# Experts' inputs: the first gathering from unsplit fp32 rows, the split parts made one pair later, two gate pieces requested earlier

## The chip, the cores and the metric

The kernel runs on one core of a Trainium2 chip. A core has a matrix engine (TensorE, PE in the profile, with its weight loads as PEld), a vector engine (VectorE, DVE), a scalar engine (ScalarE, ACT), GpSimd (POOL) and SyncE (SP), which here issues most transfers; sixteen DMA engines move the data. The metric is the device time of one execution in microseconds (us), lower is better. The given number is the median of three executions.

## The reference

The program is a small network over 256 tokens of width 1024: four layers of a first block, then two layers of a second block (layer 0 and layer 1 below). Only the end of each second-block layer matters here, its two-level mixture of experts:

```python
g_w, g_idx = lax.top_k(softmax(xf @ w_group + b_group), 1)          # one of 4 groups
e_val, e_idx = lax.top_k(e_logits of that group, 2)                 # two of its 4 experts
gates = sum(one_hot(g_idx * 4 + e_idx) * g_w * softmax(e_val))
for e in range(16):
    hid = silu(xt @ w_gate[e]) * (xt @ w_up[e])                     # 1024 -> 512
    y = y + gates[:, e:e + 1] * (hid @ w_down[e])                   # 512 -> 1024
```

All weights are fp32: 2 MB for each of the three matrices of an expert, 96 MB for the sixteen experts of a layer. Its input `xt` is a normalised, scaled and shifted copy of the layer's state.

## The kernel before, in words

**The order of the work.** The kernel is written with tile pools: a tool turns the Python program into one instruction queue for each engine, adds the waits, and chooses the order within each queue from a simulated timeline, with the order of the program as priority. Each queue runs in order. `aside`, `tick` and `settle` weave the steps of one small chain between those of another; `behind(x)` keeps an engine's instructions behind `x`. A tile is allocated from a pool under a name with a number of buffers (`one(shape, name, bufs=...)` in the stage's own pool, `wt` for the weight buffers raw, whi and wlo with four each, `xp` for xTh and xTl with two each); a buffer that is asked for again has to wait until its last reader is done, and so does a transfer into it, with all that stands behind it on SP's queue.

**The experts' stage** (`second_layer`, `moe_pass`). The tokens of an expert are gathered with matmuls: a 0/1 matrix `Dm` (128 tokens x 128 places) is made by comparing slots with an iota, and the token rows `X` (tokens on partitions) are the stationary operand, 128 features at a time. The experts are worked off in eight pairs j = 0..7 (one of the groups 0 and 1, one of the groups 3 and 2); a gathering serves two pairs, so there are four in a layer (q = 0..3), each of 4 x 2 x 2 x 2 = 32 matmuls (feature blocks, halves of the tokens, parts) of 256 columns (`collect`, line 1675). `shifted` moves the result from PSUM into `xg` on ACT (8 instructions of 128x256).

**Parts.** A row is scaled by its norm and split: `hi` is the value rounded to the engine's one-pass format fp32r, `lo` the rest. Two fp32r matmuls, with `hi` and `lo`, add up to the exact row. `parts(h)` makes both from `xG[h]`, ACT the first (line 2038), DVE the second (line 2039). The feature order is changed on the way: feature p * 8 + k goes to column k * 128 + p, because the expert weights are loaded so that each partition holds eight neighbouring rows. So the scaling reads at a stride of 8 elements, writes contiguously, and the gathering's stationary operand is contiguous.

**The routing** ahead of the first pair, for the two token halves h: update of the state, transposes, logits against the router's weights (line 2027), `route` (a chain of about a dozen short DVE instructions that finds group and experts), `route_slots` (matmuls that count earlier tokens with the same expert, line 1627), `picks` (line 1642), the first gathering with both halves apart, and `room` (counts, line 1723). `R.whose`, which `room` makes, is read by TensorE's sequencer into eight registers (line 1838) before the first expert matmul.

**A pair** (`moe_pass`, line 1829 for its matmuls in plain fp32, four experts' strips side by side): gate, up, product `t` on ACT and DVE, transposes (line 1746), down, then `leave` and in the next pair `combine` (line 1763). In pair 1 and pair 5 the next gathering (q + 1) and its place matmuls (`put`, lines 1773 and 1776) stand between the combining and the transposes; in pair 3 they stand at the end, behind a branch (line 1961) for the case that an expert has more tokens than places, which needs the parts X too and isn't taken here.

**The weights.** `expert_weights(l, name, j)` requests the four pieces (1 MB each) of one matrix of pair j. Gate pieces go to raw, but pieces 0 and 1 of odd pairs to the two xTl buffers; up goes to whi, down to wlo. Gate 0 is requested before the stage, up 0 and down 0 at its start, and those of pair j + 1 behind the matmuls of the same name of pair j. The buffer `next` holds a row for the work after the stage, loaded early.

Of the kernel before, what the change touches and what calls it, by code (L numbers as in the profile page):

```python
# [11 lines left out]
F32 = mybir.dt.float32  # L12
F32R = mybir.dt.float32r
# [3 lines left out]
OP = mybir.AluOpType  # L17
# [4 lines left out]
D = 1024  # L22
# [6 lines left out]
HALVES = (slice(0, 512), slice(512, 1024))  # L29
# [23 lines left out]
class Net:  # L53
# [1591 lines left out]
    def gather(self, R, X, sh, q, first=False):  # L1645
# [21 lines left out]
        return Dm, xg  # L1667

    def collect(self, p, X, Dm, b, halves):

        for i in range(2):
            ks = slice((2 * b + i) * 128, (2 * b + i + 1) * 128)
            for h in halves:
                for part in range(2):
                    self.nc.tensor.matmul(p[:, i], X[h][part][:, ks], Dm[:, h].rearrange("p c s -> p (c s)"),  # L1675
                                          start=h == i == part == 0, stop=h == part == 1, skip_group_check=True)

# [109 lines left out]
    def expert_weights(self, l, name, j):  # L1787


        e = [self.expert(j, s) for s in range(2)]  # L1790
        src = self.a[f"moe_w_{name}_2"][l, e[0]:e[1] + 1:e[1] - e[0]]
        pieces = []
        for i in range(4):
            if name != "down":
                tag, n, k0 = "raw" if name == "gate" else "whi", slice(0, 512), 2 * i
                s = src.rearrange("s (p i k) n -> i p s k n", i=4, k=2)[i]
            elif j < 7:
                tag, n, k0 = "wlo", slice(0, D), i
                s = src[:, 128 * i:128 * i + 128].rearrange("s (k p) n -> p s k n", k=1)
            else:  # L1800
                tag, n, k0 = "wlo", HALVES[i // 2], 2 * (i % 2)
                s = src[:, 128 * k0:128 * k0 + 256, n].rearrange("s (k p) n -> p s k n", k=2)
            if name == "gate" and j % 2 and i < 2:
                t = self.xp.tile([128, 2, 2, 512], F32, name="xTl", tag="xTl", bufs=2)
            else:
                t = self.wt(tag, [128, 2, 1 if tag == "wlo" and j < 7 else 2, n.stop - n.start], F32)
            if name == "down" and j == 7:
                for e in range(2):
                    self.nc.sync.dma_start(t[:, e], s[:, e])
            else:  # L1810
                self.nc.sync.dma_start(t, s)
            pieces.append((t, k0, n))
        return pieces

# [18 lines left out]
    def moe_pass(self, l, X, R, sh, g2, first, weights, rest, late, ahead):  # L1833
# [14 lines left out]
        for j in range(8):  # L1848
            q, c = divmod(j, 2)
            xT = xg[:, :, c * 128:(c + 1) * 128]  # L1850
            more = range(j + 1, min(j + 2, 8))
            g, u = self.pB([128, 512]), self.pB([128, 512])
# [21 lines left out]
            if j == 6:  # L1874
                late()
            DT, (gs,) = place[j]
            out[j] = DT, self.tm(dt=F32R), self.tm(dt=F32R)
            for yn, n in zip(y, HALVES):
                left = self.leave(yn, n, gs, g2, *out[j][1:])
            if j == 3:  # L1880

                self.combine(acc, range(2), j, *out.pop(j))
                rest(acc)
                Dm, xg = self.whole(self.gather(R, X, sh, q + 1))
                put(q + 1)
# [4 lines left out]
    def moe_rest(self, l, X, R, sh, g2, base, acc):  # L1890
# [15 lines left out]
        for j in range(8):  # L1906
# [6 lines left out]
            for b in range(4):  # L1913
                p = self.pB([128, 2, 128])
                for i in range(2):
                    ks = slice((2 * b + i) * 128, (2 * b + i + 1) * 128)
                    for k in range(4):
                        h, part = divmod(k, 2)
                        nc.tensor.matmul(p[:, i], X[h][part][:, ks], Dm[:, h], start=k == 0, stop=k == 3)
                self.shifted(p, xg, b, sh)  # L1920
# [18 lines left out]
    def moe(self, l, X, R, sh, g2, first, weights):  # L1939


        nc, v = self.nc, self.nc.vector
        row = self.one([128, D], "next")

        def late():
            self.bcast(self.a["final_norm_g_2"] if l else self.mod[1, D:2 * D], D, row)

# [10 lines left out]

        def rest(acc):
            n = nc.values_load(R.most, min_val=0, max_val=8)  # L1960
# [25 lines left out]

        return update, row

    def second_layer(self, l, mix, oT, after):
# [3 lines left out]
        wr, sh, row = self.routing[l]  # L1993
        y, begin, end = self.mixed(mix, oT, w, (l, 1 - l))
        weights = {"gate": self.expert_weights(l, "gate", 0)}
        g1, G = self.mod_row(l, 2), self.mod_row(l, 4)
        with self.phase(f"moe{l}", 1, 4):
            R = self.route_start()
            g2 = self.bcast(self.mod[l, 5 * D:6 * D], D, self.one([128, D], "g2"))
            for name in ("up", "down"):  # L2000
                weights[name] = self.expert_weights(l, name, 0)

            X = [[self.one([128, D], f"X{h}{part}", F32R) for part in range(2)] for h in range(2)]
            xT = self.xp.tile([128, 8, S], F32, name="xT32", tag="xTh", bufs=2)
# [14 lines left out]
            def logits(h, u):  # L2019
                p = self.pB([128, 4, 128])  # L2020
                for j in range(4):
                    k = 4 * u + j
                    nc.tensor.transpose(p[:, j], xG[h][:, k * 128:(k + 1) * 128], self.ident)
                nc.scalar.copy(xT[:, 4 * u:4 * u + 4, h * 128:(h + 1) * 128], p)
                for j in range(4):
                    k = 4 * u + j
                    nc.tensor.matmul(lgs[:, h], xT[:, k, h * 128:(h + 1) * 128], wr[:, k], start=k == 0, stop=k == 7)

            r = {}
# [37 lines left out]
            self.tick(3)  # L2067
            parts(1)
            self.settle(chain)
# [312 lines left out]
```

## Time and profile before

| | |
|---|---|
| median of three executions | 2271.1 us (2264.89 to 2271.54) |
| the profiled execution: device time | 2268.48 us |
| its span in the trace | 2266.7 us |
| TensorE busy | 2104.9 us, 93% of the span |
| weight loads (PEld) | 1608.8 us, 71% |
| DVE, ACT, POOL busy | 1346.7 us (59%), 937.4 us (41%), 25.2 us (1%) |
| mean granted clock of TensorE | 0.973 |
| HBM read | 533.36 MB, 238 GB/s over the span |

Times in the trace count from the start of the span. The experts' stage of layer 0 has its first expert matmul at 1640.27 us, that of layer 1 at 2027.24 us. Busy time of TensorE includes the pipeline's drain of each matmul, so its share is a little too high. The granted clock is 1.0 at 2.4 GHz and 0.5 at 1.2 GHz. A piece of a chain or a timeline is given by start and duration; several instructions alike that follow each other are one row with their count; in brackets stands how long the engine was idle before, and what released it.

### The profile page before, as it was taken

To read this page: it belongs to the slowest core of one execution; us is meant where nothing else is said; L and a number is where in the kernel's file an instruction comes from. 1 tells how busy PE (TensorE), PEld (TensorE's weight loads), DVE (VectorE), ACT (ScalarE), POOL (GpSimd) and SP (SyncE) were. 2 spreads that over 40 slices of the span, in tenths; PEclk is the share of its full clock that TensorE was granted. 3 is DMA by queue.
4 is the path that set the end of the run, shared out by engine and by line. 5 is a ranking of instruction groups with operands and counts; after the bars stand their busy time and mean duration, and the time that the engine had idled before them with its cause. 6 is when DMAs were issued, how large, how long until landed. Compare 5 with 4: busy or idle time off the path is not lost. (4 is left out here: it accounts for less than half of the span.)

```text
span 2266.7 us, 35540 instructions
## 1 busy us (share of the span) xinstructions
PE 2104.9 (93%) x14072; PEld 1608.8 (71%) x14072; DVE 1346.7 (59%) x2794; ACT 937.4 (41%) x1464; POOL 25.2 (1%) x69
## 2 busy tenths in 40 slices
PE   7989999989999999999999899989898988989897
PEld 5868888976788878788888698978743327864332
DVE  4578767575877665877666787677611027851112
ACT  4545435455543455544445444446411115521111
POOL 0000000000000010000000000000000001000000
PEclk9999999999999999999999999999999998999999
DMA  8527774630587464477564387656599984469995
GB/s 296 182 74 253 268 257 171 212 121 29 191 279 278 169 217 155 173 260 267 202 229 161 87 284 261 215 205 205 225 407 418 420 353 155 152 246 420 418 419 225
DMA packets 246362, 541.67 MB, mean 239 GB/s; under 512 B 27501, under 2 KB 77189, under 8 KB 246181
## 3 DMA queue, kind: packets, MB, share of 16 engines
q1 hardware_dynamic: 242597, 533.98, 65.3%
q10 hardware_dynamic: 3552, 5.24, 0.6%
q8 instruction: 116, 1.90, 0.3%
q14 instruction: 65, 0.53, 0.1%
q0 software_dynamic: 32, 0.02, 0.0%
HBM read 533.36 MB, written 5.83 MB: 238 GB/s over the span
## 5 line engine op out<-in xcount | busy, mean ns | idle before, releaser
L289 DVE TENSOR_TENSOR wlo<-raw,whi 128x1024 fp32r<-128x1024 f32 x476 | 558.5, 1221 | 223.9 <-ACT whi L270 201.8
L270 ACT CAST whi<-raw 128x2048 fp32r<-128x2048 f32 x218 | 411.1, 1907 | 417.9 <-PE pB L308 336.8
L308 PE MATMUL pB<-whi,t 128*128 128x512 f32 x1088 | 308.1, 401 | 4.7 <-ACT t L423 3.2
L308 PE MATMUL pB<-xTl,whi 128*128 128x256 f32 x1600 | 257.0, 285 | 0.0
L308 PE MATMUL pB<-xTh,whi 128*128 128x256 f32 x1600 | 254.9, 288 | 0.4 <-ACT whi L270 0.4
L308 PE MATMUL pB<-xTh,wlo 128*128 128x256 f32 x1600 | 250.2, 284 | 0.0
L308 PEld LDWEIGHTS pB<-whi,t 128*128 128x128 f32 x1088 | 202.0, 191 | 49.0 <-ACT t L423 4.1
L308 PEld LDWEIGHTS pB<-xTh,whi 128*128 128x128 f32 x1600 | 218.8, 193 | 11.8 <-issue 8.6
L308 PEld LDWEIGHTS pB<-xTl,whi 128*128 128x128 f32 x1600 | 223.2, 193 | 5.3 <-issue 2.3
L308 PEld LDWEIGHTS pB<-xTh,wlo 128*128 128x128 f32 x1600 | 217.8, 192 | 2.7 <-issue 1.7
L308 PE MATMUL pB<-wlo,t 128*128 128x512 f32 x544 | 170.9, 395 | 0.0
L308 PE MATMUL pB<-whi,xTh 128*128 128x512 f32 (+1 forms) x512 | 145.0, 409 | 11.4 <-ACT xTh L423 9.3
L308 PE MATMUL pB<-whi,xTl 128*128 128x512 f32 (+1 forms) x512 | 143.5, 402 | 10.1 <-DVE xTl L423 6.7
L308 PE MATMUL pB<-wlo,xTh 128*128 128x512 f32 (+1 forms) x512 | 139.9, 395 | 0.0
L1195 DVE SCALAR_TENSOR_TENSOR adac<-adaw,cs,adac 128x512 f32<-128x512 f32 x168 | 125.8, 749 | 21.5 <-DMA adaw<-in_w_ada_dram 19.0
L1829 PE MATMUL pB<-wlo,t 128*32 128x512 f32 (+1 forms) x1024 | 116.6, 594 | 11.7 <-ACT t L1747 11.7
L1753 DVE SCALAR_TENSOR_TENSOR t<-pB,gs,g 128x512 f32<-128x512 f32 x32 | 24.0, 751 | 166.2 <-PE pB L1829 164.6
L308 PEld LDWEIGHTS pB<-whi,xTh 128*128 128x128 f32 x512 | 95.4, 197 | 37.2 <-ACT xTh L423 15.2
L308 PEld LDWEIGHTS pB<-whi,xTl 128*128 128x128 f32 x512 | 96.9, 198 | 34.6 <-DVE xTl L423 8.7
L308 PEld LDWEIGHTS pB<-wlo,t 128*128 128x128 f32 x544 | 103.0, 189 | 24.1
L1829 PE MATMUL pB<-whi,xg 128*32 128x512 f32 (+1 forms) x1024 | 114.4, 593 | 0.0
L308 PEld LDWEIGHTS pB<-wlo,xTh 128*128 128x128 f32 x512 | 96.0, 194 | 21.6 <-issue 2.7
(384 smaller groups left out, 2375.9 us busy)
## 6 DMA issues: line engine op xcount, KB each, us to landing
raw<-in_mlp_w_dram SPq DMA_DIRECT2D x128, 1024.0 KB
whi<-in_moe_w_up_dram SPq DMA_DIRECT2D x64, 1024.0 KB
wlo<-in_moe_w_down_dram SPq DMA_DIRECT2D x56, 1024.0 KB
adaw<-in_w_ada_dram SPq DMA_DIRECT2D x96, 512.0 KB
raw<-in_moe_w_gate_dram SPq DMA_DIRECT2D x48, 1024.0 KB
raw<-in_da_w_in_dram SPq DMA_DIRECT2D x24, 1024.0 KB
raw<-in_ple_gate_w_dram SPq DMA_DIRECT2D x16, 1024.0 KB
xTl<-in_moe_w_gate_dram SPq DMA_DIRECT2D x16, 1024.0 KB
```

The source lines that it names most:

```text
L270: done = nc.scalar.copy(hi, raw)
L289: last = subtract(lo[:, ks], raw[:, ks], hi[:, ks].bitcast(F32), OP.subtract)
L308: self.last_mm = self.nc.tensor.matmul(ps, l, r, start=start and i == 0, stop=stop and i == n - 1)
L1195: v.scalar_tensor_tensor(acc, t[:, i], self.cs[:, k + i:k + i + 1], acc, op0=OP.mult, op1=OP.add)
L1753: self.nc.vector.scalar_tensor_tensor(t, p, gs, g2[:, n], op0=OP.mult, op1=OP.mult)
L1829: self.last_mm = self.nc.tensor.matmul(out[u][es], xT[:, k0 + k, es], t[:, s, k, c], start=done[u] == 1, stop=done[u] == total[u], tile_po ...
```

## The change

The scaled rows are kept once, in plain fp32 and in their natural feature order (`X`, two buffers of 128 x 1024, a third under the same name for later); the scaling reads and writes contiguously, and the subtraction is gone from the routing. The first gathering uses them unsplit, as plain fp32 matmuls with `Dm` read as fp32. All gatherings take their stationary operand at a stride of 8 elements (`some_rows`). In pair 1 the parts are made (`in_parts`): ACT copies both halves into `hi`, DVE subtracts into `lo`; the second gathering stands behind the down matmuls of pair 1 instead of before the transposes. `hi` is a buffer of 8 KB a partition that until then holds gate piece 2 of pair 1, requested at the start of the stage; gate piece 0 of pair 1 is requested by name ahead of the stage. In the second half's routing the scaling of half 0 stands behind the last copy of the transposed rows. The row for the work after the stage gets a buffer of `X` in pair 6 instead of its own. The parts are passed on to the branch.

```diff
+    def some_rows(x, k):
+        return x.rearrange("t (p k) -> t k p", k=8)[:, k]
+    def in_parts(self, X):
+        hi = self.one([128, 2, D], "hi", F32R)
+        parts = []
+        for h in range(2):
+            self.nc.scalar.copy(hi[:, h], X[h])
+            lo = self.one([128, D], "X", F32R, bufs=3)
+            self.nc.vector.tensor_tensor(lo, X[h], hi[:, h].bitcast(F32), OP.subtract)
+            parts.append([hi[:, h], lo])
+        return parts
     def collect(self, p, X, Dm, b, halves):
         for i in range(2):
-            ks = slice((2 * b + i) * 128, (2 * b + i + 1) * 128)
             for h in halves:
-                for part in range(2):
-                    self.nc.tensor.matmul(p[:, i], X[h][part][:, ks], Dm[:, h].rearrange("p c s -> p (c s)"),
...
+                places = Dm[:, h].rearrange("p c s -> p (c s)")
+                if len(X[h]) == 1:
+                    places = places.bitcast(F32)
+                for n, x in enumerate(X[h], 1):
+                    self.nc.tensor.matmul(p[:, i], self.some_rows(x, 2 * b + i), places, start=h == i == 0 and n == 1,
+                                          stop=h == 1 and n == len(X[h]), skip_group_check=True)
...
     def expert_weights(self, l, name, j):
+        return [self.asked.pop((name, j, i), None) or self.expert_piece(l, name, j, i) for i in range(4)]
+    def expert_piece(self, l, name, j, i):
...
+        elif name == "gate" and j == 1 and i == 2:
+            t = self.one([128, 2, 2, 512], "hi")
...
@@ moe_pass
-            if c and j != 3 and q < 3:
+            if j == 1:
+                X = self.in_parts(X)
+            elif c and j != 3 and q < 3:
                 Dm, xg = self.whole(self.gather(R, X, sh, q + 1))
                 put(q + 1)
             hT = self.turn(t)
...
             if j == 6:
                 late()
+            if j == 1:
+                Dm, xg = self.whole(self.gather(R, X, sh, q + 1))
+                put(q + 1)
             DT, (gs,) = place[j]
...
@@ moe
-        row = self.one([128, D], "next")
+        rows = []
         def late():
-            self.bcast(self.a["final_norm_g_2"] if l else self.mod[1, D:2 * D], D, row)
+            rows.append(self.bcast(self.a["final_norm_g_2"] if l else self.mod[1, D:2 * D], D,
+                                   self.one([128, D], "X", bufs=3)))
@@ second_layer
         weights = {"gate": self.expert_weights(l, "gate", 0)}
+        self.asked["gate", 1, 0] = self.expert_piece(l, "gate", 1, 0)
...
             g2 = self.bcast(self.mod[l, 5 * D:6 * D], D, self.one([128, D], "g2"))
+            self.asked["gate", 1, 2] = self.expert_piece(l, "gate", 1, 2)
...
-            X = [[self.one([128, D], f"X{h}{part}", F32R) for part in range(2)] for h in range(2)]
+            X = [self.one([128, D], "X", bufs=3) for h in range(2)]
...
-            def parts(h):
-                x = xG[h].rearrange("t (p k) -> t k p", k=8)
-                hi, lo = (t.rearrange("t (k p) -> t k p", k=8) for t in X[h])
-                nc.scalar.mul(hi, x, r[h])
-                v.scalar_tensor_tensor(lo, x, r[h], hi.bitcast(F32), op0=OP.mult, op1=OP.subtract)
...
-            parts(0)
             update(y1[1], 1, 1)
             chain = self.aside(rstd(1))
             for u in range(2):
-                logits(1, u)
+                copied = logits(1, u)
+            with self.behind(copied):
+                nc.scalar.mul(X[0], xG[0], r[0])
             self.settle(chain_0)
             self.route_slots(R, 0)
-            steps = self.gather(R, X, sh, 0, True)
+            steps = self.gather(R, [[x] for x in X], sh, 0, True)
...
             self.tick(3)
-            parts(1)
+            nc.scalar.mul(X[1], xG[1], r[1])
```

## Rows read from the trace of the kernel before

**Rows 1.** TensorE's waits, 2025 to 2262 us: line, released by, us in total, times, longest.

```profile
PE pB L1829 <- ACT t L1747: 5.9, 8, 0.7
PE pB L1675 <- PEq L1961: 5.8, 1, 5.8
PE pB L1763 <- ACT tm L1754: 3.5, 4, 1.5
```

**Rows 2.** Busy us by engine (x instructions), PEclk, DMA share, GB/s, one stretch.

```profile
2035.00:2235.00 200.00, 184.50 (x1574) 73.37 (x1570) 31.14 (x51) 29.05 (x60) 0.00 (x0) 0.98 1.02 417
```

**Rows 3.** Timeline of PE, layer 1's routing: start, us, operation, idle before and releaser.

```profile
2011.44 1.07 PE L2027 MATMUL pB<-rw,xT 128*128 128x24 f32 x8 [0.45 <-ACT xT L2024]
...
2019.32 2.07 PE L1675 MATMUL pB<-Dm,X 128*128 128x256 f32 x8 [1.34 <-DVE Dm L1642]
...
2023.51 0.28 PE L1723 MATMUL pB<-rmask,rc 128*128 128x16 f32 x2
...
2027.24 3.21 PE L1829 MATMUL pB<-raw,xg 128*32 x28 [1.44 <-ACT xg L1682]
```

**Rows 4.** Timeline of DVE, the same stretch.

```profile
2010.95 2.07 DVE L2039 SCALAR_TENSOR_TENSOR X<-tm,ry,X 128x1024 fp32r<-128x1024 f32 x1 [0.94 <-ACT X L2038]
2012.94 0.08 DVE L1597 MATCH_VALUE_LOAD rgi<-rgm,rlg 128x8 f32 x1
...
2013.48 2.05 DVE L2039 SCALAR_TENSOR_TENSOR X<-tm,ry,X 128x1024 fp32r<-128x1024 f32 x1
```

**Rows 5.** Line 1838, PE's register reads: x count, ns min/median/max, first and last start.

```profile
L1838 PEldq FUSED_REGOPS  x16: 146/146/165, 1637.7 to 2026.7; - x16
```

**Rows 6.** Groups of ACT and DVE by shape: x count, busy us, mean ns, idle before.

```profile
L2038 ACT ACTIVATE X<-tm,ry 128x1024 fp32r<-128x1024 f32 x4 | 8.7, 2174 | 2.2 <-DVE ry L384 2.2
L267 ACT CAST whi<-raw 128x1024 fp32r<-128x1024 f32 x8 | 7.9, 1044 | 4.8 <-PE pB L308 3.0 <-issue 1.8
...
L448 DVE SCALAR_TENSOR_TENSOR tm<-x,ry,tm 128x1024 f32<-128x1024 f32 x8 | 10.3, 1284 | 2.9 <-DMA tm<-in_norm_g_dram 2.6
...
L2039 DVE SCALAR_TENSOR_TENSOR X<-tm,ry,X 128x1024 fp32r<-128x1024 f32 x4 | 8.4, 2090 | 3.9 <-ACT X L2038 3.7
```

**Rows 7.** Timeline of PE, taps in fp32, layer 1's mixer.

```profile
1951.51 5.39 PE L1388 MATMUL pB<-glu,tm 128*128 128x256 f32 x24
```

**Rows 8.** Stretches of low granted clock in both routings, columns as in rows 2.

```profile
1627.20:1637.40 10.20, 6.26 (x28) 6.20 (x29) 8.04 (x49) 1.59 (x3) 0.00 (x0) 0.50 1.03 413
...
2012.90:2023.10 10.20, 4.37 (x19) 4.28 (x20) 8.22 (x52) 0.96 (x3) 0.00 (x0) 0.50 0.42 171
```

**Rows 9.** Timeline of DVE, layer 0's routing.

```profile
1628.52 2.05 DVE L2039 SCALAR_TENSOR_TENSOR X<-tm,ry,X 128x1024 fp32r<-128x1024 f32 x1 [0.49 <-ACT X L2038]
```

**Rows 10.** Timeline of PE, layer 0's routing.

```profile
1625.04 1.94 PE L2027 MATMUL pB<-rw,xT 128*128 128x24 f32 x16
...
1631.72 2.05 PE L1675 MATMUL pB<-Dm,X 128*128 128x256 f32 x8 [3.41 <-DVE rei L1607]
...
1636.13 0.43 PE L1723 MATMUL pB<-rmask,rc 128*128 128x16 f32 x2
...
1640.27 1.06 PE L1829 MATMUL pB<-raw,xg 128*32 x8 [1.22 <-ACT xg L1682]
```

**Rows 11.** Timeline of PE, layer 0's second pair: up, combining, gather.

```profile
1670.53 7.05 PE L1829 MATMUL pB<-whi,xg 128*32 x64
1677.51 2.12 PE L1763 MATMUL pB<-tm,DT 128*128 128x512 f32 x8
1679.47 4.00 PE L1675 MATMUL pB<-Dm,X 128*128 128x256 f32 x32
```

**Rows 12.** Timeline of PE, layer 0's third gather.

```profile
1751.14 6.83 PE L1675 MATMUL pB<-Dm,X 128*128 128x256 f32 x32 [5.73 <-PEq L1961]
```

**Rows 13.** Timeline of SP's issues, layer 0 and layer 1.

```profile
1588.11 0.46 SPq L1811 DMA_DIRECT2D xTl<-in_moe_w_gate_dram  x1
...
2005.20 0.47 SPq L1811 DMA_DIRECT2D wlo<-in_moe_w_down_dram  x1
```

More of the change, by code (lines that the diff above doesn't have):

```diff
@@ L1667, in gather @@
         return Dm, xg
+    @staticmethod
+    def some_rows(x, k):
[9 more added lines that the diff above has]
+        return parts
     def collect(self, p, X, Dm, b, halves):
         for i in range(2):
-            ks = slice((2 * b + i) * 128, (2 * b + i + 1) * 128)
             for h in halves:
-                for part in range(2):
-                    self.nc.tensor.matmul(p[:, i], X[h][part][:, ks], Dm[:, h].rearrange("p c s -> p (c s)"),
-                                          start=h == i == part == 0, stop=h == part == 1, skip_group_check=True)
+                places = Dm[:, h].rearrange("p c s -> p (c s)")
[4 more added lines that the diff above has]
+                                          stop=h == 1 and n == len(X[h]), skip_group_check=True)
     def shifted(self, p, xg, b, sh):
@@ L1787, in expert_weights @@
     def expert_weights(self, l, name, j):
+        return [self.asked.pop((name, j, i), None) or self.expert_piece(l, name, j, i) for i in range(4)]
+    def expert_piece(self, l, name, j, i):
         e = [self.expert(j, s) for s in range(2)]
         src = self.a[f"moe_w_{name}_2"][l, e[0]:e[1] + 1:e[1] - e[0]]
[L1792 to L1812, printed above, removed]
@@ L1813, in expert_weights @@
-        return pieces
+        if name != "down":
+            tag, n, k0 = "raw" if name == "gate" else "whi", slice(0, 512), 2 * i
+            s = src.rearrange("s (p i k) n -> i p s k n", i=4, k=2)[i]
+        elif j < 7:
+            tag, n, k0 = "wlo", slice(0, D), i
+            s = src[:, 128 * i:128 * i + 128].rearrange("s (k p) n -> p s k n", k=1)
+        else:
+            tag, n, k0 = "wlo", HALVES[i // 2], 2 * (i % 2)
+            s = src[:, 128 * k0:128 * k0 + 256, n].rearrange("s (k p) n -> p s k n", k=2)
@@ new lines, in expert_piece @@
+        if name == "gate" and j % 2 and i < 2:
+            t = self.xp.tile([128, 2, 2, 512], F32, name="xTl", tag="xTl", bufs=2)
+        elif name == "gate" and j == 1 and i == 2:
+            t = self.one([128, 2, 2, 512], "hi")
+        else:
+            t = self.wt(tag, [128, 2, 1 if tag == "wlo" and j < 7 else 2, n.stop - n.start], F32)
+        if name == "down" and j == 7:
+            for e in range(2):
+                self.nc.sync.dma_start(t[:, e], s[:, e])
+        else:
+            self.nc.sync.dma_start(t, s)
@@ L1815, in experts @@
+        return t, k0, n
     def experts(self, xT, pieces, whose, out):
@@ L1882, in moe_pass @@
                 self.combine(acc, range(2), j, *out.pop(j))
-                rest(acc)
+                rest(acc, X)
                 Dm, xg = self.whole(self.gather(R, X, sh, q + 1))
@@ L1915, in moe_rest @@
                 for i in range(2):
-                    ks = slice((2 * b + i) * 128, (2 * b + i + 1) * 128)
                     for k in range(4):
                         h, part = divmod(k, 2)
-                        nc.tensor.matmul(p[:, i], X[h][part][:, ks], Dm[:, h], start=k == 0, stop=k == 3)
+                        nc.tensor.matmul(p[:, i], self.some_rows(X[h][part], 2 * b + i), Dm[:, h], start=k == 0,
+                                         stop=k == 3)
                 self.shifted(p, xg, b, sh)
@@ L1957, in ahead, with rest @@
                 self.low_parts.append((self.early[k], raw))
-        def rest(acc):
+        def rest(acc, X):
             n = nc.values_load(R.most, min_val=0, max_val=8)
@@ L1985, in update @@
             self.squares(h, u)
-        return update, row
+        return update, rows[0]
     def second_layer(self, l, mix, oT, after):
@@ L1994, in second_layer @@
         y, begin, end = self.mixed(mix, oT, w, (l, 1 - l))
+        self.asked = {}
         weights = {"gate": self.expert_weights(l, "gate", 0)}
+        self.asked["gate", 1, 0] = self.expert_piece(l, "gate", 1, 0)
         g1, G = self.mod_row(l, 2), self.mod_row(l, 4)
@@ L2023, in logits @@
                     nc.tensor.transpose(p[:, j], xG[h][:, k * 128:(k + 1) * 128], self.ident)
-                nc.scalar.copy(xT[:, 4 * u:4 * u + 4, h * 128:(h + 1) * 128], p)
+                last = nc.scalar.copy(xT[:, 4 * u:4 * u + 4, h * 128:(h + 1) * 128], p)
                 for j in range(4):
@@ L2027, in logits @@
                     nc.tensor.matmul(lgs[:, h], xT[:, k, h * 128:(h + 1) * 128], wr[:, k], start=k == 0, stop=k == 7)
+                return last
             r = {}
```

## The prediction

> **What bounds the kernel now.** The page first: TensorE is busy over nine tenths of the span (the table above). The change touches only the two expert stages, one for each layer of the second block, so they are read by themselves. In the second one the waits of TensorE name ACT, DVE and its own sequencer, never a transfer [rows 1], although the DMA engines are full for the whole stretch, at 417 GB/s and a share of 1.02 [rows 2]. So weights arrive as fast as they can and still in time: DMA is full because it runs ahead into free buffers, and TensorE sets the end. What lengthens or shortens TensorE's own line counts in full; what makes weights arrive earlier does not.
>
> Ahead of each stage lies a chain of small steps (logits, route, slots, pick matrices, first gather). There DVE sets the pace: in layer 1 TensorE's logits are out at 2012.5, yet the first gather starts at 2019.32 [rows 3], because two long DVE subtractions of 2.07 and 2.05 us stand among the route's steps [rows 4]. The end of that chain is neither the gather nor its eviction but TensorE's sequencer, which reads eight expert numbers one after another (last at 2026.7) [rows 5]; the experts start at 2027.24, 3.73 us after the count matmul of line 1723 began at 2023.51 [rows 3].
>
> **The change part by part.**
>
> *Parts taken out of the routing, layer 1.* One contiguous scaling per half replaces a strided scaling and a strided subtraction. DVE loses the two subtractions and its waits for ACT; ACT's scaling falls from 2174 ns to about the 1044 ns of a contiguous copy of the same size [rows 6]. Without the two blocks the route goes on at 2010.0 (the first block's 0.94 us of idle time begins there) instead of 2012.94; the steps that then ran, 0.5 us before the second block and 3.8 us from its end at 2015.53 to the gather, need 4.3 us at most, less when not interleaved [rows 3, 4]. First gather at about 2014.1, 5.2 us earlier.
>
> *First gather in fp32.* 16 matmuls replace 32, but an fp32 matmul runs as two passes: one channel group's 31 taps of line 1388, fp32 with the same 128x256 shape, are 62 instructions, and 24 of them take 5.39 us, 0.215 us a pass without the last one's drain [rows 7]. So 32 passes of 0.215 us at the full clock, 6.9 us instead of 3.8, and double that at the low clock. The granted clock is 0.50 (the 1.2 GHz level) in this stretch and rose 3.8 us after the first gather began in layer 1, 5.7 us in layer 0 [rows 8, 3, 10]. Layer 1 after: 8 passes at 0.43 = 3.4 us to 2017.5; slot matmuls 0.7 to 2018.2; 8 passes, the clock rising between 2017.9 and 2019.8, so 1.7 to 2.5 us, to 2019.9 to 2020.7. There the count matmul runs, at 2023.51 before. Behind it stand the 3.73 us of register reads, and the other 16 passes (3.4 us, and 0.3 for the count) fit beside them. Gain 2.8 to 3.6 us, taken 3.2.
>
> *Layer 0.* There only the second subtraction was in the way: 2.05 us, and 0.49 of waiting [rows 9]. The gather starts at some 1629.3 instead of 1631.72; 3.4 us, 0.7 us and 1.7 to 2.6 us later the count matmul comes at 1635.1 to 1636.0, before at 1636.13 [rows 10]. The start of the experts at 1640.27 moves by -1.2 to 0, taken -0.6. If the clock rose later than before, this would be a loss of up to 1.5 us. Both layers: -3.8 (-4.8 to -1).
>
> *Strided weights.* The scaled rows now lie in their natural order, and every gather takes its 128 stationary columns 8 elements (32 bytes) apart. No row of before has a strided weight load, so the price is bounded. Below: nothing. Above: the strided scaling itself reads at this stride, 2174 against 1044 ns on ACT, 1.10 ns an element; on DVE 2090 against 1284 ns, 0.79 ns an element [rows 6]. For 128 columns that is 141 or 101 ns a load. A load alone paces 0.111 us (16 of line 2027, of 24 columns, in 1.94 us) [rows 10], and a pair of load and 256-column matmul 0.120 us (32 in 4.00, less the drain) [rows 11]. So the load already sets the pace and nothing hides an addition. I take the smaller of the two, 101 ns, nearer to the cheap end: the pair grows to 0.22 us. In the first gather it stays under the 0.215 us pass. The gathers for the second and fourth pair run at the full clock: 2 x 2 x 32 = 128 loads x 0.101 = 12.9 us. The third pair's gather runs mostly at the low clock, 0.213 us a pair (32 in 6.83) [rows 12], which the longer load just fits; its last loads give 0.5 us in each layer. Sum +13.9 (0 to +26, the top with 141 ns and a load that doubles at the low clock too).
>
> *Parts made while the second pair runs.* Two ACT copies of 1.04 us and two DVE subtractions of about 1.3 us [rows 6] in each layer. They wait for the gate piece that held their buffer, which is used up when the 7.05 us of the up matmuls begin [rows 11]; ACT and DVE have one short step each in those, so the 4.7 us are hidden. Were they put behind the product instead, the down matmuls would wait up to 2.6 us a layer. The gather itself moves from before the transposes to behind the down matmuls: the same instructions. While DVE and ACT make the product, pair 0's combining (2.1 us) still covers them, as it ran ahead of the gather before [rows 11]; the gather's eviction gets the place matmuls as cover, as the third pair's has. Taken 0 (-1 to +3).
>
> *Early pieces.* The piece of pair 1 that is named first was already issued at 1588.11, ahead of the stage [rows 13]; only the other one is new. It moves 1 MB, 2.5 us at 417 GB/s, from the full stretch into an idle one. Since TensorE waits for no transfer, 0. On SP's queue it stands before the eight up and down pieces, the last of which was issued at 2005.20 [rows 13]; at 2.5 us each they are in by 2025.2 at the latest, and the up matmuls start some 7 us behind 2027.24, so a late buffer costs nothing below 9 us. The later broadcast of 512 KB is 1.3 us of transfer in the full stretch: 0 for the same reason.
>
> *Sum.* -3.8 + 13.9 + 0 + 0 = +10.1 on the profiled execution's 2268.5 us (span 2266.7 and 1.8 around it): 2278.6 us. That execution is 2.6 us below the median of the runs shown, 2271.1; I give 2279.
>
> **The rivals.**
>
> *A, strided loads cost nothing* (the one on the other side). Then -3.8 remains: 2264.7. Its place is the pair of 0.120 us; it decides as soon as the added price is under 0.03 us a load (3.8 / 128). For it: a matmul's moving side takes 256 columns in no more time than a load needs for 128, so TensorE's reads may have room. Against it: two engines slow down at this very stride. The Trainium skill, "TensorE: Matmul & The Clock Gate", section "LDWEIGHTS (loading the stationary operand)", gives a load's time by its columns alone; that agrees with the 0.111 us for contiguous columns and would give this case, 2264.7. The Trainium skill, "SBUF — State Buffer", section "Door 1: The DMA port swizzle", says that accesses which each open a new 16-byte line pay; ACT's doubling agrees, no run yet shows it for TensorE.
>
> *B, the early piece pays.* If transfers do hold TensorE back in a way that the waits don't show, 2.5 us a layer come on top of A: 2259.7. The full DMA speaks for it, rows 1 against it.
>
> *C, the dear end of the stride:* 128 x 0.141 = 18 and about 8 us in the third pair's gathers, less 3.8: +22, 2290.7. For it: the ACT row.
>
> **How the numbers follow.** Forecast (2273 to 2286 by itself) 0.45, A 0.33, B 0.12, C 0.10. A difference under 0.3%, 6.8 us, can't be told from none. The forecast is slower in 0.32 and the same in 0.13 (its low end is +5); A the same in 0.23 and faster in 0.10 (with a larger gain in the routing); B faster in 0.11 and the same in 0.01; C slower in 0.10. Together faster 0.21, same 0.37, slower 0.42. The range from 2260 to 2290 leaves out half of B and half of C.
>
> **What would show it.** Right: the gather in pair 1's stretch takes about 7 us for 32 loads instead of 4.0, with weight loads some 100 ns longer; the first gather has 32 fp32 passes of 0.215 us or more; between the last logits and the experts layer 1 is 3 us shorter and layer 0 hardly. Wrong: later gathers that still pace 0.120 us; a first gather that runs at the low clock to its end, which delays the experts; a wait of the second pair's down matmuls for ACT or DVE; an expert stage that ends earlier than its start and its gathers explain, which would be B.

## The result and the profile after

The changed kernel takes 2287.4 us in the median of five executions (2285.75 to 2288.82), the kernel before 2271.1 us (2264.89 to 2273.98): ratio 1.0075, 95% interval 1.006 to 1.0091. It is slower by 16.3 us by the medians. The profiled execution took 2285.75 us, its span is 2284.0 us, 17.3 us more than before; it is accounted for below.

The weight loads of all gathers (ns: least, median, largest), before in the first row and after in the others, then TensorE's timeline in layer 0 from the second gather to pair 2's transposes, then the third gather in layer 1 and its clock before and after 2153.85 us (columns as in rows 2; timelines: start, us, operation, idle before and releaser):

```profile
L1675 PEld LDWEIGHTS pB<-Dm,X x256: 186/192/338, 1631.7 to 2189.5; 128*128 128x128 f32 x128
L1693 PEld LDWEIGHTS pB<-Dm,X x160: 312/337/347, 1627.2 to 2206.6; 128*128 128x128 f32 x160
L1693 PEld LDWEIGHTS pB<-Dm,hi x96: 312/338/347, 1685.4 to 2206.4; 128*128 128x128 f32 x96
```

```profile
1685.38 0.52 PE L1693 MATMUL pB<-Dm,hi 128*128 128x256 f32 x1
1685.73 0.41 PE L1693 MATMUL pB<-Dm,X 128*128 128x256 f32 x1
1685.98 0.41 PE L1693 MATMUL pB<-Dm,hi 128*128 128x256 f32 x1
...
1691.35 0.63 PE L1781 MATMUL pB<-tm,DT 128*128 128x512 f32 x2
1691.82 0.29 PE L1693 MATMUL pB<-Dm,hi 128*128 128x256 f32 x1
...
1693.63 1.09 PE L1781 MATMUL pB<-tm,DT 128*128 128x512 f32 x4
...
1711.19 0.63 PE L1764 MATMUL pB<-ident,t 128*128 128x128 f32 x4 [0.90 <-DVE t L1883]
```

```profile
2149.61 0.57 PE L1693 MATMUL pB<-Dm,hi 128*128 128x256 f32 x1 [5.71 <-PEq L1987]
...
2150.23 0.44 PE L1693 MATMUL pB<-Dm,hi 128*128 128x256 f32 x1
2150.47 0.44 PE L1693 MATMUL pB<-Dm,X 128*128 128x256 f32 x1
...
2157.14 0.41 PE L1693 MATMUL pB<-Dm,X 128*128 128x256 f32 x1
2157.39 0.60 PE L1791 MATMUL pB<-ident,Dm 128*128 128x128 f32 x4
```

```profile
2149.60:2153.80 4.20, 4.19 (x17) 4.20 (x18) 0.20 (x2) 0.45 (x2) 0.00 (x0) 0.50 1.03 413
2153.90:2157.30 3.40, 3.40 (x16) 3.40 (x16) 0.00 (x0) 1.98 (x5) 0.00 (x0) 1.00 0.94 382
```

Three things are to be seen. The second gather [rows 11] now goes at 0.245 us a pair of load and matmul instead of 0.120; from its start to what follows it fills 7.78 us, 1685.38 to 1691.35 and 1691.82 to 1693.63, where 3.83 did (4.00 with the drain). The eight matmuls between its parts are pair 1's combining; it has moved in here from pair 2, and pair 2's transposes now wait 0.90 us for DVE. And the third gather [rows 12] goes at 0.24 us a pair at the low clock as well as at the full one behind it.

The routings, TensorE in layer 0 and layer 1, the stretches of low clock (columns as in rows 2), and the new scalings:

```profile
1622.86 1.94 PE L2056 MATMUL pB<-rw,xT 128*128 128x24 f32 x16
...
1627.21 3.78 PE L1693 MATMUL pB<-Dm,X 128*128 128x256 f32 x8 [1.07 <-DVE rei L1607]
...
1633.38 0.47 PE L1741 MATMUL pB<-rmask,rc 128*128 128x16 f32 x2
1633.71 4.18 PE L1693 MATMUL pB<-Dm,X 128*128 128x256 f32 x16
1637.83 7.07 PE L1849 MATMUL pB<-raw,xg 128*32 x64
...
2018.24 1.94 PE L2056 MATMUL pB<-rw,xT 128*128 128x24 f32 x16 [0.43 <-DVE ry L384]
...
2022.62 3.78 PE L1693 MATMUL pB<-Dm,X 128*128 128x256 f32 x8 [1.10 <-DVE Dm L1642]
...
2028.96 0.47 PE L1741 MATMUL pB<-rmask,rc 128*128 128x16 f32 x2
2029.29 4.18 PE L1693 MATMUL pB<-Dm,X 128*128 128x256 f32 x16
2033.40 7.08 PE L1849 MATMUL pB<-raw,xg 128*32 x64
```

```profile
1624.80:1631.60 6.80, 4.98 (x15) 4.23 (x15) 4.40 (x35) 1.24 (x3) 0.00 (x0) 0.50 1.03 417
2020.80:2027.60 6.80, 5.57 (x16) 4.76 (x17) 4.29 (x35) 0.42 (x2) 0.00 (x0) 0.50 0.86 355
```

```profile
L2083 ACT ACTIVATE X<-tm,ry 128x1024 f32<-128x1024 f32 x2 | 2.3, 1164 | 0.0
```

The gather stands right behind the logits and the steps of the route; no long DVE block is between them any more. Then it takes longer: from its start to the count matmul 6.17 us in layer 0 and 6.34 in layer 1, where it took 4.41 and 4.19 [rows 10, 3]. Behind the count, 16 passes of 0.240 us end only 4.4 us later, and the experts start with them.

To compare runs, three lengths are read from each trace: from the start of the last logits matmul (0.27 us before the end of its row) to the first expert matmul; from there to the end of the last combining (the stage); and the pace of the second gather.

| kernel | experts start, layer 0 / 1 | stage, layer 0 / 1 | second gather, pace |
|---|---|---|---|
| before | 13.56 / 14.99 us | 231.80 / 229.17 us | 0.120 us |
| changed | 13.30 / 13.49 | 242.48 / 240.25 | 0.245 |

One trace was taken of each kernel. In the five of this document whose routing is that of the changed kernel, layer 0's start lies between 13.29 and 13.36 us, but layer 1's between 13.16 and 13.86; there a difference of less than 0.7 us tells nothing.

In layer 1, 0.6 us more is gained ahead of the last logits: DVE's last update step, on which nothing of the change acts, stands 8.29 us later than before, the last logits 7.67. The first row is of before, the second of after:

```profile
2005.15 0.70 DVE L2011 TENSOR_TENSOR pB<-pB,tm 128x512 f32<-128x512 f32 x1 [0.25 <-PE pB L308]
```

```profile
2013.44 0.70 DVE L2040 TENSOR_TENSOR pB<-pB,tm 128x512 f32<-128x512 f32 x1 [0.26 <-PE pB L308]
```

### The profile page after: what moved, and what is told of

It is laid out like the page before. It is cut to its first block, busy times and chain, and to the rows that moved or that the text cites. A ratio compares the mean times of both kernels' runs of the same rounds, so it can differ in the third digit from the quotient of the medians.

```text
span 2284.0 us, 35545 instructions
## 1 busy us (share of the span) xinstructions
PE 2130.1 (93%) x14072; PEld 1630.4 (71%) x14072; DVE 1343.8 (59%) x2794; ACT 940.0 (41%) x1468; POOL 24.6 (1%) x69
```

## Experiments

Each ratio is to executions of the kernel before that were taken beside the run, with medians of 2267.4 to 2269.0 us; so kernels are to be compared by their ratios and stages and not by their times alone.

### The weights' gap

*Contiguous parts.* The edit, and what was expected:

```diff
-            self.nc.scalar.copy(hi[:, h], X[h])
+            x = X[h].rearrange("t (p k) -> t k p", k=8)
+            split = lambda t: t.rearrange("t (k p) -> t k p", k=8)
+            self.nc.scalar.copy(split(hi[:, h]), x)
...
-            self.nc.vector.tensor_tensor(lo, X[h], hi[:, h].bitcast(F32), OP.subtract)
+            self.nc.vector.tensor_tensor(split(lo), x, split(hi[:, h]).bitcast(F32), OP.subtract)
```

> The changed kernel, but hi and lo are written with the 128 features of each block next to each other (ACT and DVE read the unsplit row at the stride instead), so the later gathers load contiguous columns; the first gather keeps its stride. Stride theory: the gathers of the second and fourth pair go back from 0.242 to 0.120 us a pair of load and matmul (7.8 to 3.8 us each), the third pair's by 1 to 2 us; in all 4 x 3.95 + 3.1 = 19 us less than the changed kernel, near 2267 us by the profiled execution, if ACT's two copies (1.04 to about 2.2 us) and DVE's two subtractions (1.3 to 2.1 us) stay hidden beside pair 1. Rival, the place: the gathers are slow because they now stand behind the down matmuls and read hi, which shares its buffer with a gate piece; then the pace stays 0.24 and the time 2286. Second rival: the longer copies come out from under the second pair's matmuls, up to 2 x 1.9 us a layer; then 2271 to 2275.

Measured: 2266.34 us, ratio 0.9992 (0.9983 to 1.0001). The second gather takes 3.92 us, 0.120 a pair, at its new place and from the same `hi`; the stages are 233.26 and 230.32 us, 9.2 and 9.9 less than the changed kernel's. The copies and subtractions doubled, and no wait came of it:

```profile
L1681 ACT CAST hi<-X 128x1024 fp32r<-128x1024 f32 x4 | 8.3, 2124 | 7.4 <-PE pB L1851 7.4
L1683 DVE TENSOR_TENSOR X<-X,hi 128x1024 fp32r<-128x1024 f32 x4 | 8.3, 2087 | 10.5 <-ACT hi L1681 10.2
```

So the gap of the weights alone holds 19.1 us of the loss, and the gather's new place none of its slower pace. What the stages still take more than before, 1.46 and 1.15 us, has another cause (the cover of pair 2, below).

*The kernel before in natural order.* From the other side:

```diff
-                x = xG[h].rearrange("t (p k) -> t k p", k=8)
-                hi, lo = (t.rearrange("t (k p) -> t k p", k=8) for t in X[h])
+                x, (hi, lo) = xG[h], X[h]
...
-                    self.nc.tensor.matmul(p[:, i], X[h][part][:, ks], Dm[:, h].rearrange("p c s -> p (c s)"),
+                    self.nc.tensor.matmul(p[:, i], X[h][part].rearrange("t (p k) -> t k p", k=8)[:, 2 * b + i], Dm[:, h].rearrange("p c s -> p (c s)"),
```

> The kernel before, but the scaled parts stay in their natural feature order, so that all gatherings, the first too, load columns 8 elements apart; nothing else of the change is in it. Stride theory: gathers of the second and fourth pair 7.8 us instead of 3.8 to 4.4, the third pair's 7.8 instead of 5.9 to 6.7, in all +19 us; the contiguous scaling and subtraction give back 1.1 us each on ACT and 0.8 us each on DVE in the routing, of which 1 to 3 us a layer count: 2282 to 2286. Rival, the place: no change in the gathers' pace, and only the gain in the routing, 2263 to 2267.

Measured: 2282.93 us, ratio 1.0066 (1.005 to 1.0081); stages 240.67 and 238.72 us, 8.9 and 9.6 more than before. The second gather, in its old place, with its drain:

```profile
1676.12 7.76 PE L1675 MATMUL pB<-Dm,X 128*128 128x256 f32 x32
```

The same price without anything else of the change. The experts start at 12.77 and 14.09 us, 0.8 and 0.9 earlier than before: that much the contiguous scaling and subtraction give back, with the first gather's slower loads already in it. In layer 0 this is 0.5 us earlier than the changed kernel's 13.30, although the split is still in the routing; so all of the changed kernel's gain there comes with the contiguous reading, and the unsplit gather takes part of it back. In layer 1 the changed kernel starts 0.6 us earlier, which is inside the scatter named above.

*Gaps of 2 and 4 elements.* `gap` is 2 in layer 0, 4 in layer 1:

```diff
-        return x.rearrange("t (p k) -> t k p", k=8)[:, k]
+        return x.rearrange("t (a p b) -> t a b p", a=8 // s, b=s)[:, k // s, k % s]
```

> The changed kernel, but hi and lo lie so that neighbouring columns of a block are 2 elements (8 bytes) apart in layer 0 and 4 elements (16 bytes) in layer 1, instead of 8 elements (32 bytes) in both. Three laws for the load's price: a step (any gap costs the full price): 0.24 us a pair in both layers, time as the changed kernel's, 2286. In proportion to the distance: 0.120 + 0.122 x (gap - 1) / 7, so 0.137 and 0.172 us, 2271 to 2276. By lines of 16 bytes, each paid once: at 4 elements each column opens its own line and the price is the full 0.24 us; at 2 elements two columns share one, so about 0.12 us; layer 0 then takes some 9 us less than the changed kernel and layer 1 the same, 2277. The page on the state buffer of the Trainium skill (SBUF — State Buffer, section Door 1: The DMA port swizzle) has the rule of lines.

Measured: 2274.43 us, ratio 1.0031 (1.0019 to 1.0043). The stages are 233.35 us in layer 0, 9.1 less than the changed kernel's, and 239.54 in layer 1, 0.7 less. The time alone lies in the range that was given for the proportion, 2271 to 2276; the loads decide. Those of the second gather (ns: least, median, largest), layer 0, then layer 1, and two matmuls of each:

```profile
L1696 PEld LDWEIGHTS pB<-Dm,hi x16: 195/195/198, 1684.9 to 1688.9; 128*128 128x128 f32 x16
...
L1696 PEld LDWEIGHTS pB<-Dm,hi x16: 309/329/334, 2071.1 to 2078.4; 128*128 128x128 f32 x16
```

```profile
1685.09 0.28 PE L1696 MATMUL pB<-Dm,X 128*128 128x256 f32 x1
1685.21 0.28 PE L1696 MATMUL pB<-Dm,hi 128*128 128x256 f32 x1
...
2071.66 0.40 PE L1696 MATMUL pB<-Dm,hi 128*128 128x256 f32 x1
2071.89 0.40 PE L1696 MATMUL pB<-Dm,X 128*128 128x256 f32 x1
```

8 bytes apart a pair takes 0.120 us, as if contiguous; 16 bytes apart 0.233; 32 bytes apart 0.242. Neither the step at any gap nor the proportion (0.137 and 0.172) holds; the price starts between 8 and 16 bytes and hardly grows after that. The Trainium skill, "SBUF — State Buffer", section "Door 1: The DMA port swizzle", says that two accesses to a 16-byte line are needed to hide the latency and that each access to a new line pays; that is what these loads show. The Trainium skill, "TensorE: Matmul & The Clock Gate", section "LDWEIGHTS (loading the stationary operand)", gives a load's time by its columns alone; that holds here at 8 bytes and no longer at 16.

### The cover of pair 2

```diff
             if j - 1 in out:
-                self.combine(acc, range(2), j - 1, *out.pop(j - 1))
+                with self.behind(*[self.last_mm] * (j == 2)):
+                    self.combine(acc, range(2), j - 1, *out.pop(j - 1))
```

> The changed kernel, but the combining of pair 1 is held behind the last up matmul of pair 2, where it stood in the kernel before, instead of standing inside the second gather. Cover theory: in the changed kernel the product of pair 2 has no matmuls beside it, so TensorE waits 0.90 us for DVE, and pair 3's combining, split over the up matmuls, costs 0.43 us more; held back, the wait of 0.90 us ahead of pair 2's transposes goes, 0.95 to 1.4 us a layer, 2 to 2.8 us in all (2283 to 2284). Rival: the wait comes from DVE being late with the parts or the gather's work rather than from the missing cover; then it stays, with the combining's 2 us only moved, and the time stays at 2286.

Measured: 2284.4 us, ratio 1.0075 (1.0061 to 1.0088). The times can't tell the difference from the changed kernel; the stages can: 241.64 and 239.45 us, 0.84 and 0.80 less. In layer 1 the experts start 0.37 us later (13.86), which is inside the scatter. Layer 0, up, combining and transposes of pair 2:

```profile
1697.30 7.05 PE L1849 MATMUL pB<-whi,xg 128*32 x64
1704.28 2.12 PE L1781 MATMUL pB<-tm,DT 128*128 128x512 f32 x8
1706.24 0.60 PE L1764 MATMUL pB<-ident,t 128*128 128x128 f32 x4
```

The wait of 0.90 us is gone, without DVE's work having changed (the last product step takes 0.69 us in both): the missing cover made it. Pair 3's combining is still split over the up matmuls, and its price stays: in layer 0 from pair 2's transposes to pair 3's 25.49 us, with 25.52 in the changed kernel and 25.16 before, so some 0.35 us and not 0.43.

### What the early piece does

```diff
-        elif name == "gate" and j == 1 and i == 2:
-            t = self.one([128, 2, 2, 512], "hi")
...
-            self.asked["gate", 1, 2] = self.expert_piece(l, "gate", 1, 2)
```

> The changed kernel without the new early request: gate piece 2 of pair 1 goes to a raw buffer in its old place in the queue, and hi has its buffer to itself. Theory that TensorE waits for no transfer: the stages from the first expert matmul to the last combining stay at 242.5 and 240.3 us, no wait for a DMA appears, and the time is that of the changed kernel (ratio to before near 1.0075). Rival: the early piece pays its 2.5 us of transfer in each layer; taken away, the stages grow by up to 2.5 us each, ratio near 1.0095.

Measured: 2290.4 us, ratio 1.0094 (1.0077 to 1.011), as the rival had it, yet not for its reason. No matmul of the stages waits for a transfer. The stage of layer 1 is 240.12 us; that of layer 0 is 243.68, because the last 32 down matmuls took 5.34 us instead of 3.64 at a low granted clock (second row: columns as in rows 2):

```profile
1877.61 5.34 PE L1847 MATMUL pB<-wlo,t 128*32 x32
1877.80:1881.20 3.40, 3.40 (x20) 0.87 (x16) 1.57 (x3) 1.45 (x4) 0.00 (x0) 0.50 0.08 22
```

These 1.7 us stand at the same place in the traces of three other runs below, and in none of the rest; why the clock fell in these four is open. What is late besides is the start of the experts, 14.09 and 15.21 us. DVE in layer 0's routing:

```profile
1630.20 0.48 DVE L1642 TENSOR_SCALAR Dm<-rslots,rslot 128x128 fp32r<-128x128 f32 x2
1630.89 1.22 DVE L1681 TENSOR_TENSOR X<-X,hi 128x1024 fp32r<-128x1024 f32 x1
1632.02 0.48 DVE L1642 TENSOR_SCALAR Dm<-rslots,rslot 128x128 fp32r<-128x128 f32 x2
1635.70 0.88 DVE L1642 TENSOR_SCALAR Dm<-rslots,rslot 128x128 fp32r<-128x128 f32 x4
1637.43 1.22 DVE L1681 TENSOR_TENSOR X<-X,hi 128x1024 fp32r<-128x1024 f32 x1 [0.85 <-PE pB L1693]
1638.57 0.15 DVE L1745 TENSOR_SCALAR whose<-pB 1x8 int32<-1x8 f32 x1
```

With `hi` free, the subtractions stand among the pick matrices and right ahead of `whose`: the blocks that the change had taken out of the routing are back. Two runs were to show whether this is all that the piece does. The first ordered the parts behind pair 0's last down matmul:

```diff
+            if j == 1:
+                with self.behind(self.last_mm):
+                    X = self.in_parts(X)
```

> The kernel without the early request of gate piece 2, but the making of the parts is held behind the last down matmul of pair 0 by an explicit order. In the run without the request the copies and the first subtractions (1.22 us each on DVE) had moved up into the routing, two of them ahead of pick matrices and of the step that makes the experts' numbers, and the experts started 14.1 and 15.2 us behind the last logits matmul instead of 13.3 and 13.5. Theory that the piece only held back the parts, by occupying their buffer: the start returns to 13.3 and 13.4 us, the stages to 242.5 and 240.3, and the ratio to before to 1.0075. Rival, that the early transfer itself is what counts: the start stays at 14 and 15 us, or a wait for a transfer shows, and the ratio stays near 1.0094.

Measured: 2289.89 us, ratio 1.0096 (1.008 to 1.0111), start 14.06 and 15.28 us, stages 243.63 and 241.88, each with 1.7 us under a low granted clock (in layer 1 0.61 from 2112.4 to 2116.0 us). This told nothing of the two theories: the order given against a matmul left the parts of ACT and DVE in the routing. The second gave the order on the engines themselves:

```diff
-                with self.behind(self.last_mm):
+                with self.behind(*left):
```

> Again without the early request of gate piece 2, now with the making of the parts ordered on ACT and DVE themselves, each behind its own last step for pair 0's outputs (an order given against a matmul had not moved them: they still stood in the routing). Theory that the piece only held back the parts: the experts start 13.3 and 13.4 us behind the last logits matmul as in the changed kernel (14.1 and 15.3 with the parts in the routing), stages 242.5 and 240.3, ratio to before 1.0075. Rival, that the early transfer is what counts: 14 and 15 us, or a wait for a transfer in the second pair, ratio near 1.0095.

Measured: 2284.71 us, ratio 1.0081 (1.0068 to 1.0093); start 13.36 and 13.69 us, stages 242.20 and 240.18. DVE, layer 0:

```profile
1628.18 0.15 DVE L1745 TENSOR_SCALAR whose<-pB 1x8 int32<-1x8 f32 x1 [1.01 <-PE pB L1741]
1658.22 2.56 DVE L1681 TENSOR_TENSOR X<-X,hi 128x1024 fp32r<-128x1024 f32 x2 [0.25 <-ACT hi L1679]
```

Without the early piece and with the parts out of the routing, start and stages are the changed kernel's to 0.3 us. The piece is worth nothing as a transfer that these stages show; by occupying `hi` it keeps 0.8 and 1.7 us out of the routing.

### Versions without the price

All four write the scaled rows from the start with a gap of 2 elements, and read them at that gap in every gather. The last three do without the early piece and have the second gather in its old place; the second diff is that of the first of these, in the others the parts are ordered as in the two runs above:

```diff
-        return x.rearrange("t (p k) -> t k p", k=8)[:, k]
+        return x.rearrange("t (a p b) -> t a b p", a=4, b=2)[:, k // 2, k % 2]
...
-                nc.scalar.mul(X[0], xG[0], r[0])
+                nc.scalar.mul(X[0].rearrange("t (a p b) -> t a p b", a=4, b=2), xG[0].rearrange("t (p a b) -> t a p b", a=4, b=2), r[0])
```

```diff
-            if j == 1:
+            if j == 0:
                 X = self.in_parts(X)
...
-            if j == 1:
-                Dm, xg = self.whole(self.gather(R, X, sh, q + 1))
-                put(q + 1)
             DT, (gs,) = place[j]
```

With the combining held:

> The changed kernel, but the scaled rows are written from the start with neighbouring columns of a block 2 elements apart (so every gather, the first too, loads at this gap), and the combining of pair 1 is held behind pair 2's up matmuls. If a load at this gap is free for fp32 passes too: 0.215 us a pass instead of 0.240 at the full clock in the first gather, the experts start 12.9 us behind the last logits matmul instead of 13.3 to 13.5; ACT's scaling, which now reads 8 bytes at a time, stays near 1.2 us; the stages take 232.4 and 229.5 us (those with contiguous parts, 233.3 and 230.3, less 0.8 each). Together some 2.4 us under the kernel with contiguous parts, near 2264. Rival: ACT's scaling costs 2.1 us as at a gap of 8 elements and delays the first gather, or the fp32 passes pay for the gap; then the first gather stays as it is and 0.8 us a layer are left, 2265 to 2266.

Measured: 2264.22 us, ratio 0.9983 (0.9974 to 0.9992); start 12.92 and 12.99 us, stages 232.64 and 230.57. As expected in the routing: 16 passes behind the count take 3.70 us with their drain instead of 4.18, and ACT's scaling is 1.24 us although it reads pairs of elements. The stage of layer 1 was expected at 229.5; 1.0 of the 1.1 us that it missed by stand in the third gather, 6.63 us against 5.64 with contiguous parts, as the granted clock stayed at 0.50 longer. Layer 1:

```profile
2020.13 0.47 PE L1741 MATMUL pB<-rmask,rc 128*128 128x16 f32 x2
2020.46 3.70 PE L1693 MATMUL pB<-Dm,X 128*128 128x256 f32 x16
```

```profile
L2084 ACT ACTIVATE X<-tm,ry 128x1024 f32<-128x1024 f32 x2 | 2.5, 1238 | 0.0
```

With the parts made in pair 0 and the second gather in its old place, and with the parts ordered behind pair 0's last down matmul:

> As the kernel with rows 2 elements apart, but the parts are made in pair 0, the second gather stands ahead of pair 1's transposes where it stood in the kernel before, no combining is held and no gate piece is asked for early: of the change only the unsplit first gather is left. If the routing's gain and the second gather's place are independent: experts 12.9 us behind the last logits matmul (before 13.6 and 15.0), stages as before, 231.8 and 229.2 us; 0.7 and 2.1 us less than before, ratio 0.9988. Rival: the two copies and two subtractions in pair 0 get in the way of its product or of its outputs' scaling, up to 4.5 us a layer; then the stages grow and the kernel is no faster than before.

> Rows 2 elements apart from the scaling on, the unsplit first gather, no early piece, the parts held behind pair 0's last down matmul, and the second gather back ahead of pair 1's transposes. If the parts are done beside pair 1's gate and up matmuls: experts start 12.9 to 13.0 us behind the last logits matmul (before 13.6 and 15.0), stages as before, 231.8 and 229.2 us. 0.6 and 2.0 us less than before and 2.2 us less than the version with the held combining; ratio to before near 0.998. Rival: the gather ahead of the transposes waits for the second subtraction, or pair 1's up product for ACT, up to 2 us a layer; then it is level with that version or slower.

Measured: 2269.0 us, ratio 1.0004 (0.9994 to 1.0014), and 2268.38 us, 0.9998 (0.9988 to 1.0008). Both missed at the same points: the parts ran in the routing, the experts started at 13.95 and 15.13 us, and at 13.84 and 15.11; and the stages, expected as before, were 233.50 and 230.12, and 233.53 and 230.09. The 1.7 us in layer 0 are the low clock under the last down matmuls again: pair 7's transposes still stand within 0.05 us of before, counted from the start of the stage. So this is not the rival's price of work in pair 0. With the order on the engines themselves:

> Rows 2 elements apart from the scaling on, unsplit first gather, no early piece, the parts ordered on ACT and DVE behind pair 0's outputs, the second gather ahead of pair 1's transposes. Experts 12.9 to 13.0 us behind the last logits matmul, stages as before, 231.8 and 229.2 us: 2.7 us less than before and some 2 less than the version with the held combining, ratio near 0.9978. Rival: with the parts beside pair 1's gate matmuls its product or the gather has to wait for ACT or DVE, up to 2 us a layer, and it is level with that version.

Measured: 2263.56 us, ratio 0.9985 (0.9976 to 0.9994); start 12.94 and 13.37 us, stages 231.83 and 229.12, those of before. This version and the one with the held combining are 0.15 and 0.17% faster than the kernel before, with intervals that stay below a ratio of 1, and can't be told from each other.

## Why the prediction was right, and where its sizes were off

The sum was +10.1 us on the profiled execution; the stretches that it speaks of grew by 19.3 us, nearly twice as much. The rest of the program was 2.1 us faster up to layer 0's routing; hence 17.3 us of span. That is scatter and not the change: DVE's last update step ahead of layer 0's routing stands at 1621.6 us before, 1619.4 after, and between 1613.7 and 1623.1 in the eleven traces of the experiments, whose edits touch no step of TensorE, ACT or DVE up to there. So the time came this near to the forecast by luck in part. The median, 2287.4, lies above the forecast's own range, 2273 to 2286, and inside the wide one, 2260 to 2290.

| term | predicted | measured (rounded) |
|---|---|---|
| routing, layer 0 / 1 | -0.6 / -3.2 us | -0.3 / -2.1 us |
| gap, second and fourth gathers | +12.9 | +15.9 |
| gap, third gathers | +1.0 | +3.1 |
| parts and the moved gather | 0 | +2.8 |
| early pieces as transfers | 0 | 0 |

*Parts taken out of the routing.* Right, though the run of the kernel before in natural order shows that in layer 0 the contiguous reading alone gains more than the whole change. With 8.29 us taken off, the first gather of layer 1 starts at 2014.3, forecast 2014.1, and the count matmul runs at 2020.7, forecast 2019.9 to 2020.7; in layer 0, with the 2.1 us added, 1629.3 and 1635.5, forecast 1629.3 and 1635.1 to 1636.0. The clock rose as the second 8 passes began (at 1631.6 and 2027.6 us), as assumed. What failed is that the other 16 passes "fit beside" the register reads: at 0.240 us instead of 0.215 they end after them, 4.44 us from the count to the experts instead of 3.73. That is 0.7 us, and 0.3 in layer 0 (4.45 instead of 4.14).

*Strided weights.* Right in mechanism and sign, mis-sized. The forecast took the smaller of two engines' prices, 0.101 us, for the load; it is 0.122, between them, so 15.9 us instead of 12.9 (3.95 and 4.04 in layer 0, twice 3.95 in layer 1). In the third gather the load was thought to fit under the low clock's 0.213 us a pair; it takes 0.24, so each pair costs 0.03 there, and the pairs behind the clock's rise 0.12: 1.2 and 1.9 us instead of 0.5 each. Rival A, loads without a price, fell with the contiguous parts: they alone brought back 19.1 us.

*Parts made while the second pair runs.* Hidden, as forecast: even at 2.1 us each they made no wait. The step that failed is "the same instructions" for the moved gather. It looked for the cover of pair 1's product and of the gather's eviction, and not for what else had stood in the gap: the gather at its new place drew pair 1's combining into it, pair 2's product lost its cover (the stretch up to pair 2's transposes is 1.05 us a layer longer than the gather's price explains, 0.90 of it the wait), and pair 3's combining was split (0.35). The held combining brought back 0.8 of it a layer; the price of the split is read from the timelines, and no run removed it alone.

*Early pieces.* Costed at nothing as a transfer, rightly, and rival B fell with that. The forecast did say that the parts wait for the piece in `hi`, but took this wait for harmless and not for useful: it is what keeps the parts out of the routing, and without it 2.5 us of the routing's gain would have been lost.

The forecast, 2278.6 us for the profiled execution that took 2285.75, is right in sign and 7.1 us short; rival C, at 2290.7, priced the single load dearer than it is and came nearer to the time by luck: it had no term for the lost cover either, and the two errors stand against each other.

## What to carry to other kernels

Before a rearrangement is moved from a vector engine to a matmul's stationary operand, look at the distance of neighbouring columns: here 8 bytes cost nothing and 16 or 32 doubled the time of a load with its matmul, and a layout with pairs side by side gave the scaling and the loads nearly all of the contiguous speed. When a block of matmuls is moved, list what its neighbours were covering, as a combining that goes along can leave a product bare in the next pair. And work that has been taken off a chain can come back into it when its buffer is free: in four runs here the parts did, and an order on their own engines kept them away.

## What the hardware showed that was not expected

The load with a gap of 32 bytes paces 0.24 us at the 1.2 GHz level and at 2.4 GHz alike (third gather above), while the contiguous pair takes 0.213 and 0.120. So the gap costs 0.12 us at the full clock and 0.03 at the low one, and 0.025 where a pass of 0.215 us already hides most of the load.

ACT and DVE, too, pay when they read single elements and hardly for pairs: pairs of elements out of 32 bytes (layer 0 of the run with gaps of 2 and 4) took ACT 2.26 us for both copies, four elements out of 32 bytes 1.99 us in layer 1, and single elements 4.2 us (2 x 2124 ns, contiguous parts; a contiguous copy of this size takes 1044 ns in the changed kernel). DVE's subtractions took 1225 ns each at pairs and at fours, and 2087 ns at single elements.

```profile
1666.13 2.26 ACT L1682 CAST hi<-X 128x1024 fp32r<-128x1024 f32 x2 [3.71 <-PE pB L1852]
2052.36 1.99 ACT L1682 CAST hi<-X 128x1024 fp32r<-128x1024 f32 x2 [3.71 <-PE pB L1852]
```
